# Copies of the forgetting heads from ScalarE to GpSimd, and one row tile's count from VectorE to ScalarE

## The chip, the cores and the metric

The kernel runs on one core of one Trainium2 chip. The metric is the time of one execution on the device in microseconds (us), lower is better. The engines are TensorE (PE in the profile, its weight loads PEld), VectorE (DVE), ScalarE (ACT), GpSimd (POOL) and SyncE (SP), which issues most DMAs.

## The reference

One decoder block on a sequence of 1024 rows of width 1024. The input is normalised and modulated, and one large projection of it gives queries, keys and values of eight forgetting heads and eight sparse heads, an indexer, and two gates. The forgetting heads are causal attention with a decay, the sparse heads attend to 256 keys that the indexer selects, and a gated merge and an MLP follow.

```python
h = rmsnorm(x, g_norm1) * (1.0 + scale1) + shift1
proj = h @ w_in
...
    s = jnp.einsum('bqhd,bkhd->bhqk', qb, k).astype(jnp.float32) * scale
    s = s + Fb[..., :, None] - Ft[:, :, None, :]
    s = jnp.where(mask[None, None], s, -jnp.inf)
    p = jax.nn.softmax(s, axis=-1).astype(v.dtype)
...
    iscore = jnp.where(causal[None], iscore, -jnp.inf)
    _, sel = lax.top_k(iscore, topk)        # topk = 256
...
merged = (jax.nn.sigmoid(gate_fox) * (y_fox @ w_branch_fox)
          + jax.nn.sigmoid(gate_dsa) * (y_dsa @ w_branch_dsa))
x = x + gate1 * (merged @ w_out)
x = x + gate2 * (jnp.square(jax.nn.relu(h2 @ w_mlp1)) @ w_mlp2)
```

## The kernel before

Every product is made from operands split in two halves: a high half `hi`, the value rounded to TensorE's fast 32-bit format, and a low half `lo`, the rest. Three matmuls (`hi*hi`, `hi*lo`, `lo*hi`) stand for one. Weights come by DMA into a staging tile `st` (three buffers), and `split_st` makes `whi` (a copy, L117, on ScalarE) and `wlo` (a difference, L118, on GpSimd for most weights). Both have two buffers.

After a first stage (normalisation, transposes, the indexer's scores), a loop runs over sixteen heads, eight forgetting heads (`n < NH`) and then eight sparse ones. Each turn has the head's `attention`, the next head's projection `proj_qk`, every second turn the values of two heads (`proj_v`), and one or two gate tiles (`gate_tile`), which are 48 matmuls of 128x512 each and fill TensorE between the steps of attention. In `proj_qk` a product of 512 columns in a PSUM bank `g` holds 64 rows of the query and 64 of the key. The score needs the query's high half twice (upper and lower 64 partitions of `QA`), and the key's high half in `KA` and in `KB`: ScalarE makes four copies of 64x512 from the bank (L308, L309, L312, L313), and VectorE the two differences (L310 `QB`, L314 `KA`), of which the last frees the bank.

In the turns of the forgetting heads the kernel also finds the 256th largest indexer score of each row, by 32 steps of bisection (`bisect_step`, four per turn in the code) and one extra count between the two halves of the bits. A step takes a candidate threshold (`cand`, `nct`), counts for each of six row tiles (2 to 7, of 384 to 1024 columns) how many scores reach it, compares (`cnt` with `goal`, L507) and updates the threshold. `count` gives the last `NA` row tiles to ScalarE (L484, a sign with an accumulated sum) and the others to VectorE (L487). `select_tile` (L516 to L524, VectorE alone, with a scan at L521) then makes the masks that the sparse heads need.

Tiles, buffers and semaphores are managed by a framework. It also sets the order on each engine: a planner places the instructions by the program's order of priorities and its own costs, so an instruction stands in its engine's queue where the planner expects it to be ready, and each queue is then worked off in order. Changed costs or engines therefore move the instructions of a whole stage. SyncE's DMA queue is fed in the same way.

Of the kernel before, what the change touches and what calls it, by code (L numbers as in the profile page):

```python
# [9 lines left out]
F32 = mybir.dt.float32  # L10
# [6 lines left out]
AF = mybir.ActivationFunctionType  # L17
# [8 lines left out]
NTT = S // P  # L26
HD = 64
NH = 8
# [29 lines left out]
def block_kernel(ctx: ExitStack, tc: tile.TileContext, x, c, w_ada, b_ada, g_norm1, w_in, b_forget,  # L58
                 rel_bias, w_bf, w_bd, w_out, g_norm2, w_mlp1, w_mlp2, g_final, onehot, out):
    nc = tc.nc  # L60
# [3 lines left out]
    def pool(stack, name, bufs=1, **kw):  # L64
        if kw.get("space") != DRAM:
            kw.setdefault("reuse_waits", "tile")
        return stack.enter_context(tc.tile_pool(name=name, bufs=bufs, **kw))
# [37 lines left out]
    R_d = drm.tile([2, D], F32, name="R_d")  # L105


    def split_w(pieces, lo_eng=None, kt=KT, dst=None):
        st = stg.tile([P, 1024], F32, name="st", tag="st")
        view = st.rearrange("p (k c) -> p k c", k=kt)  # L110
        for d0, d1, src in pieces:
            nc.sync.dma_start(view[:, :, d0:d1], src)
        return split_st(st, lo_eng, dst)

    def split_st(st, lo_eng=None, dst=None):
        hi, lo = dst or [wts.tile([P, 1024], F32R, name=n, tag=n) for n in ("whi", "wlo")]
        nc.scalar.activation(hi, st, AF.Copy)  # L117
        (lo_eng or nc.vector).tensor_tensor(lo, st, hi.bitcast(F32), op=ALU.subtract)  # L118
        return hi, lo

# [70 lines left out]
    with ExitStack() as st1:  # L191
# [38 lines left out]
        with tc.high_priority():  # L230
            for kb, (kt0, n) in enumerate(KBS):
                if kb:
                    was = load_ada(kt0, n)
                for j, wt in was:
                    acc = p1.tile([P, 256], F32, name="acc", tag=f"acc{j}")[:, 0:n * P]
                    if j == 1 and kb < 2:
                        ps = ppv.tile([P, 512], F32, name="pv", tag="pv")
# [17 lines left out]
                for k in range(kt0, kt0 + n):  # L255
                    for g in range(2):
                        gs = slice(g * 512, (g + 1) * 512)
                        ps = ptr.tile([P, 512], F32, name="xT", tag="tr")
# [35 lines left out]
    def proj_qk(kind, h):  # L294
        cq, ck = (C_QF, C_KF) if kind == 0 else (C_QD, C_KD)
        cq, ck = cq + h * HD, ck + h * HD
        hi, lo = split_w([(0, 64, win[:, :, cq:cq + HD]), (64, 128, win[:, :, ck:ck + HD])], nc.gpsimd)
        QA = pQ.tile([P, S], F32R, name="QA", tag="QA", bufs=2)
        QB = pQ.tile([P, S], F32R, name="QB", tag="QB", bufs=2)
        KA = pQ.tile([P, S], F32R, name="KA", tag="KA", bufs=2)  # L300
        KB = pQ.tile([P, S], F32R, name="KB", tag="KB", bufs=2)
        nc.sync.dma_start(QB[64:68, :].bitcast(F32), E_d[kind * NH + h, 0:4, :].bitcast(F32))
        nc.sync.dma_start(KB[64:68, :].bitcast(F32), E_d[kind * NH + h, 4:8, :].bitcast(F32))
        sc = -(HD ** -0.5)
        for half in range(2):
            sl = slice(half * 512, half * 512 + 512)
            ps = gemm_h(hi, lo, half)
            nc.scalar.activation(QA[0:64, sl], ps[0:64, :], AF.Copy, scale=sc)  # L308
            nc.scalar.activation(QA[64:128, sl], ps[0:64, :], AF.Copy, scale=sc)  # L309
            nc.vector.scalar_tensor_tensor(QB[0:64, sl], ps[0:64, :], sc, QA[0:64, sl].bitcast(F32),  # L310
                                           op0=ALU.mult, op1=ALU.subtract)
            nc.scalar.activation(KA[64:128, sl], ps[64:128, :], AF.Copy)  # L312
            nc.scalar.activation(KB[0:64, sl], ps[64:128, :], AF.Copy)  # L313
            nc.vector.tensor_tensor(KA[0:64, sl], ps[64:128, :], KA[64:128, sl].bitcast(F32), op=ALU.subtract)  # L314
        return QA, QB, KA, KB

# [130 lines left out]


    pA = pool(at_stack, "pA")
    NQ, NA = NTT - 2, 2  # L450
    Thi = pA.tile([P, NQ], F32, name="Thi")
    Tlo = pA.tile([P, NQ], F32, name="Tlo")
    cand = pA.tile([P, NQ], F32, name="cand")
# [263 lines left out]

    for n, (kind, h) in enumerate(heads):
        qk = qk_next
        if h % 2 == 0:  # L720
            V = V_next
        attention(kind, h, qk, V[h % 2], Yd)
        if n + 1 < len(heads):
            qk_next = proj_qk(*heads[n + 1])
        if h % 2 == 1 and n + 1 < len(heads):
            V_next = proj_v(heads[n + 1][0], heads[n + 1][1] // 2)
        for g in GATES.get(n, ()):
            gate_tile(g)
        if n < NH:
            for b in range(4):  # L730
                if bit == 15:
                    bisect_mid()
                bisect_step(bit)
                bit -= 1
        if NH <= n + 1 < 2 * NH:
            ada_later(n + 1 - NH)
        if n == NH - 1:
            for i in range(2, NTT):
                select_tile(i)
        if n == 3:  # L740
            dsa_consts()
        for piece in PIECES.get(n, ()):
            branch_fox(piece)
        if n == 2 * NH - 2:
            h_stack.close()
            pYd = pool(yd_stack, "pYd", side="right")
            Yd = [pYd.tile([P, 4, S], F32R, name=f"Yd{v}") for v in range(2)]
            pY = pool(yd_stack, "pY", side="right")
    for v in range(2):
        load_y(Yd[v], 1, v, range(3), slice(0, S))  # L750
        load_y(Yd[v], 1, v, (3,), slice(0, S), slice(0, 64))
# [10 lines left out]
    for half in range(2):  # L762
        sl = slice(half * 512, half * 512 + 512)
        for cp in range(4):
            hi, lo = split_w([(0, 256, wbv[1][:, :, cp * 256:cp * 256 + 256])], nc.gpsimd, 4)
            hv, lv = hi.rearrange("p (k c) -> p k c", k=4), lo.rearrange("p (k c) -> p k c", k=4)
            for c2 in range(2):
# [5 lines left out]
                ps = bank("q")  # L773
# [217 lines left out]
    with ExitStack() as st5:  # L991
# [108 lines left out]
        ps = run(step_24)  # L1100
# [102 lines left out]
```

## Time and profile before

| what | value |
|---|---|
| median of 3 runs | 1655.07 us (1651.3 to 1658.26) |
| the profiled execution | 1651.19 us, span of its instructions 1649.4 us |
| TensorE busy in the span | 1573.0 us (95%) |
| VectorE busy | 1168.3 us (71%) |
| ScalarE busy | 958.9 us (58%) |
| GpSimd busy | 690.7 us (42%) |
| mean granted TensorE clock | 0.982 of full speed |

The forgetting heads' attention runs from about 153 us, where the first score matmul of head 0 starts, to about 531 us, where that of the first sparse head starts. The ends of matmuls are modelled in the trace, so a high busy share of TensorE doesn't yet mean that it works at its best pace; how many matmuls start in a stretch tells more.

### The profile page before, as it was taken

What the parts mean: (1) busy time and instruction counts of PE and PEld (TensorE: products, weight loads), DVE (VectorE), ACT (ScalarE), POOL (GpSimd) and SP (SyncE); (2) the same over time, 40 slices, a digit from 0 to 9 for tenths busy, and PEclk for the clock granted to TensorE, in tenths of its full rate; (3) what the DMA queues carried; (4) which work ended last, traced back from release to release, by engine and by line L of the source; (5) the groups of instructions that cost most, each with busy time, mean ns of one, the idle gap of its engine ahead of it and who ended that gap; (6) DMA issues with size and microseconds to landing.
All of it is one profiled execution on the core that took longest, in us unless ns stands there. A gap on an engine that the chain in (4) does not pass through costs nothing.

```text
span 1649.4 us, 22813 instructions
## 1 busy us (share of the span) xinstructions
PE 1573.0 (95%) x7585; PEld 1302.1 (79%) x7585; DVE 1168.3 (71%) x2293; ACT 958.9 (58%) x1678; POOL 690.7 (42%) x573
## 2 busy tenths in 40 slices
PE   4989999998889999999999998999999989999998
PEld 3767787786678888888887887888888868888887
DVE  6787999999954566556667546765555475758988
ACT  4467898898467777677763135555454343533433
POOL 3421121121122574756655211777766553334730
PEclk7999999999999999999999999999999989999999
DMA  9221122222232444445778455554444479665862
GB/s 301 78 59 57 45 75 56 51 66 50 75 78 65 127 129 113 122 143 152 267 276 271 157 171 203 161 168 159 148 159 141 179 263 354 228 213 191 269 217 103
DMA packets 223870, 253.02 MB, mean 153 GB/s; under 512 B 49136, under 2 KB 136256, under 8 KB 223752
## 3 DMA queue, kind: packets, MB, share of 16 engines
q1 hardware_dynamic: 215112, 233.73, 44.9%
q10 hardware_dynamic: 8640, 17.83, 2.8%
q8 instruction: 60, 0.98, 0.3%
q14 instruction: 58, 0.48, 0.1%
HBM read 186.48 MB, written 65.03 MB: 152 GB/s over the span
## 4 chain that ended last, share of the span: by engine, by line
PE 71%; DVE 16%; ACT 5%; DMA 3%; issue 3%; POOL 1%; SPq 1%; ACTq 0%; DVEq 0%; POOLq 0%
PE g L75 32%; PE S L75 21%; PE tr L75 8%; PE pv L75 7%; DVE bjunk L487 2%; PE ptr L572 2%; DVE ut L1026 2%; DVE acc L247 1%; ACT eqt L484 1%; DVE sp L552 1%; DVE pl L574 1%; ACT sp L559 1%; DMA gt<-G_d 1%; DVE C L1085 1%; ACT sp L556 1%
## 5 line engine op out<-in xcount | busy, mean ns | idle before, releaser
L118 POOL TENSOR_TENSOR wlo<-st,whi 128x1024 fp32r<-128x1024 f32 x60 | 147.6, 2461 | 304.5 <-ACT whi L117 269.5
L75 PE MATMUL g<-h_hi,whi 128*128 128x512 f32 x656 | 265.3, 404 | 7.7 <-DVE KA L314 5.8
L75 PE MATMUL g<-h_hi,wlo 128*128 128x512 f32 x656 | 263.1, 401 | 0.0
L75 PE MATMUL g<-h_lo,whi 128*128 128x512 f32 x656 | 262.0, 399 | 0.0
L1026 DVE TENSOR_TENSOR ut<-rw,ut 128x1024 fp32r<-128x1024 f32 x112 | 185.6, 1701 | 65.9 <-ACT ut L1025 65.5
L1025 ACT ACTIVATE ut<-rw 128x1024 fp32r<-128x1024 f32 x112 | 112.0, 1051 | 141.9 <-PE pv L75 66.8
L1040 POOL TENSOR_TENSOR rw<-rw 128x1024 f32<-128x1024 f32 x40 | 112.1, 2807 | 132.7 <-DMA rw<-in_w_mlp_dram 120.8
L75 PEld LDWEIGHTS g<-h_hi,whi 128*128 128x128 f32 x656 | 125.4, 191 | 33.4 <-DVE KA L314 3.6
L75 PEld LDWEIGHTS g<-h_hi,wlo 128*128 128x128 f32 x656 | 125.2, 191 | 24.4
L75 PEld LDWEIGHTS g<-h_lo,whi 128*128 128x128 f32 x656 | 125.1, 191 | 23.5
L75 PE MATMUL S<-ut 128*128 128x512 f32 (+1 forms) x576 | 138.3, 384 | 0.0
L75 PEld LDWEIGHTS S<-ut 128*128 128x128 f32 x576 | 106.6, 191 | 21.5 <-DVE ut L1026 0.4
L117 ACT ACTIVATE whi<-st 128x1024 fp32r<-128x1024 f32 x74 | 78.0, 1054 | 70.0 <-PE g L75 21.4
L574 DVE TENSOR_TENSOR pl<-ptr,ph 128x512 fp32r<-128x512 f32 (+1 forms) x160 | 99.4, 630 | 24.2 <-ACT ph L573 19.8
L556 ACT ACTIVATE sp<-sp,mn 128x128 f32<-128x128 f32 (+7 forms) x128 | 98.5, 771 | 30.4 <-DVE mn L552 30.1
L573 ACT ACTIVATE ph<-ptr 128x512 fp32r<-128x512 f32 (+1 forms) x160 | 86.0, 551 | 49.4 <-PE ptr L572 46.8
L559 ACT ACTIVATE sp<-sp,mn 128x128 f32<-128x128 f32 (+7 forms) x128 | 96.8, 770 | 18.4 <-DVE mn L558 18.1
L487 DVE TENSOR_SCALAR_CACHE_REDUCE bjunk<-sel_all,cand 128x384 bf16<-128x384 int16 (+7 forms) x132 | 106.3, 805 | 1.4
L572 PE MATMUL ptr<-ident,sp 128*128 128x128 f32 x576 | 91.7, 275 | 9.4 <-DVE pl L574 9.4
L75 PE MATMUL g<-ut 128*128 128x512 f32 (+1 forms) x384 | 94.7, 382 | 6.3 <-ACT ut L1025 4.6
L75 PE MATMUL pv<-ph,V 128*128 128x256 f32 x320 | 86.4, 290 | 1.7 <-DVE yt L581 0.9
L75 PEld LDWEIGHTS g<-ut 128*128 128x128 f32 x384 | 70.0, 191 | 21.1 <-ACT ut L1025 5.0
(433 smaller groups left out, 3873.7 us busy)
## 6 DMA issues: line engine op xcount, KB each, us to landing
rw<-in_w_mlp_dram SPq DMA_DIRECT2D x72, 512.0 KB
rw<-U_d SPq DMA_DIRECT2D x56, 512.0 KB
wap<-in_w_ada_dram SPq DMA_DIRECT2D x64, 256.0 KB
st<-in_w_mlp_dram SPq DMA_DIRECT2D x32, 512.0 KB
st<-in_w_in_dram SPq DMA_DIRECT2D x26, 512.0 KB
U_d<-cc SPq DMA_DIRECT2D x48, 256.0 KB
st<-in_w_in_dram SPq DMA_DIRECT2D x33, 256.0 KB
G_d<-t SPq DMA_DIRECT2D x32, 256.0 KB
```

The lines of the kernel that those rows point to most:

```text
L75: nc.tensor.matmul(o, l, r, start=start, stop=stop)
L117: nc.scalar.activation(hi, st, AF.Copy)
L118: (lo_eng or nc.vector).tensor_tensor(lo, st, hi.bitcast(F32), op=ALU.subtract)
L487: nc.vector.tensor_scalar(bjunk[:, :(i + 1) * P], sel[i].bitcast(dt), thr[:, q], None, op0=ALU.is_ge, op1=ALU.add, accum_out=cnt[:, q])
L556: nc.scalar.activation(sp[:, :W], sp[:, :W], AF.Exp, bias=mn[:, len(cs) - 1:len(cs)], scale=-1.0, accum_out=mn[:, 2:3])
L559: nc.scalar.activation(sp[:, :W], sp[:, :W], AF.Copy, scale=mn[:, 3:4])
L572: nc.tensor.transpose(tr[:, n * P:(n + 1) * P], pt[s][:, kb * P:(kb + 1) * P], ident)
L573: nc.scalar.activation(ph[:, z:], tr[:, z:], AF.Copy)
L574: nc.vector.tensor_tensor(pl[:, z:], tr[:, z:], ph[:, z:].bitcast(F32), op=ALU.subtract)
L1025: nc.scalar.activation(ut[:, n], t, AF.Copy)
L1026: nc.vector.tensor_tensor(ut[:, n + 1], t, ut[:, n].bitcast(F32), op=ALU.subtract)
L1040: nc.gpsimd.tensor_tensor(o, a, b, op=op)
```

## The change

While the loop is in a forgetting head's turn (`n < NH`), three kinds of copies are made by GpSimd: the weights' high half `whi`, the second copy of the query's high half (`QA[64:128]`) and the copy of the key's high half in `KB`. The last two now read the first copy in SBUF, where ScalarE read the PSUM bank. `NA` becomes 3, so ScalarE counts row tile 5 (768 columns) too, and VectorE three tiles in place of four. `on_pool` is set as a turn begins, ahead of its projections and gates, so the first head's projections, made before the loop, are as they were. In all 23 copies of `whi` and 32 of the 64x512 copies go to GpSimd, and 33 counts go from VectorE to ScalarE.

```diff
--- before.py
+++ after.py
@@ -105,6 +105,8 @@
     R_d = drm.tile([2, D], F32, name="R_d")
 
 
+    on_pool = [False]
+
     def split_w(pieces, lo_eng=None, kt=KT, dst=None):
         st = stg.tile([P, 1024], F32, name="st", tag="st")
         view = st.rearrange("p (k c) -> p k c", k=kt)
@@ -114,7 +116,10 @@
 
     def split_st(st, lo_eng=None, dst=None):
         hi, lo = dst or [wts.tile([P, 1024], F32R, name=n, tag=n) for n in ("whi", "wlo")]
-        nc.scalar.activation(hi, st, AF.Copy)
+        if on_pool[0]:
+            nc.gpsimd.tensor_copy(hi, st)
+        else:
+            nc.scalar.activation(hi, st, AF.Copy)
         (lo_eng or nc.vector).tensor_tensor(lo, st, hi.bitcast(F32), op=ALU.subtract)
         return hi, lo
 
@@ -306,11 +311,17 @@
             sl = slice(half * 512, half * 512 + 512)
             ps = gemm_h(hi, lo, half)
             nc.scalar.activation(QA[0:64, sl], ps[0:64, :], AF.Copy, scale=sc)
-            nc.scalar.activation(QA[64:128, sl], ps[0:64, :], AF.Copy, scale=sc)
+            if on_pool[0]:
+                nc.gpsimd.tensor_copy(QA[64:128, sl], QA[0:64, sl].bitcast(F32))
+            else:
+                nc.scalar.activation(QA[64:128, sl], ps[0:64, :], AF.Copy, scale=sc)
             nc.vector.scalar_tensor_tensor(QB[0:64, sl], ps[0:64, :], sc, QA[0:64, sl].bitcast(F32),
                                            op0=ALU.mult, op1=ALU.subtract)
             nc.scalar.activation(KA[64:128, sl], ps[64:128, :], AF.Copy)
-            nc.scalar.activation(KB[0:64, sl], ps[64:128, :], AF.Copy)
+            if on_pool[0]:
+                nc.gpsimd.tensor_copy(KB[0:64, sl], KA[64:128, sl].bitcast(F32))
+            else:
+                nc.scalar.activation(KB[0:64, sl], ps[64:128, :], AF.Copy)
             nc.vector.tensor_tensor(KA[0:64, sl], ps[64:128, :], KA[64:128, sl].bitcast(F32), op=ALU.subtract)
         return QA, QB, KA, KB
 
@@ -447,7 +458,7 @@
 
 
     pA = pool(at_stack, "pA")
-    NQ, NA = NTT - 2, 2
+    NQ, NA = NTT - 2, 3
     Thi = pA.tile([P, NQ], F32, name="Thi")
     Tlo = pA.tile([P, NQ], F32, name="Tlo")
     cand = pA.tile([P, NQ], F32, name="cand")
@@ -717,6 +728,7 @@
 
     for n, (kind, h) in enumerate(heads):
         qk = qk_next
+        on_pool[0] = n < NH
         if h % 2 == 0:
             V = V_next
         attention(kind, h, qk, V[h % 2], Yd)
@@ -746,6 +758,7 @@
             pYd = pool(yd_stack, "pYd", side="right")
             Yd = [pYd.tile([P, 4, S], F32R, name=f"Yd{v}") for v in range(2)]
             pY = pool(yd_stack, "pY", side="right")
+    on_pool[0] = False
     for v in range(2):
         load_y(Yd[v], 1, v, range(3), slice(0, S))
         load_y(Yd[v], 1, v, (3,), slice(0, S), slice(0, 64))
```

The planner orders every queue anew. Three places show it. The first is GpSimd's queue just ahead of the small copies of `dsa_consts` in the fourth turn. `wlo` is the weights' low half, `ph` and `pl` are zeroed blocks of the attention's probabilities. Before:

```order
L568 MEMSET ph 128x128
L569 MEMSET pl 128x128
L118 TENSOR_TENSOR wlo<-st,whi 128x1024
L568 MEMSET ph 128x128
L569 MEMSET pl 128x128
L118 TENSOR_TENSOR wlo<-st,whi 128x1024
```

With the change (a CAST is the copy, L120 of the weights, L315 of the query, L322 of the key):

```order
L322 CAST KB<-KA 64x512
L120 CAST whi<-st 128x1024
L579 MEMSET ph 128x128
L580 MEMSET pl 128x128
L315 CAST QA<-QA 64x512
L123 TENSOR_TENSOR wlo<-st,whi 128x1024
L322 CAST KB<-KA 64x512
L579 MEMSET ph 128x128
L580 MEMSET pl 128x128
L120 CAST whi<-st 128x1024
L123 TENSOR_TENSOR wlo<-st,whi 128x1024
```

Each `wlo` now has its `whi` ahead of it in the same queue, and the query's and key's copies stand between.

The second place is ScalarE's queue around the projection of the third head (`sp` is a softmax tile, `yt` and `yh` the head's output, `ptr` transposed probabilities). Before:

```order
L308 ACTIVATE QA<-g 64x512
L309 ACTIVATE QA<-g 64x512
L484 ACTIVATE eqt,cnt<-sel_all,nct 128x1024
L556 ACTIVATE sp,mn<-sp,mn 128x1024
L580 ACTIVATE yt<-pv 64x256
L573 ACTIVATE ph<-ptr 128x512 x2
L312 ACTIVATE KA<-g 64x512
L313 ACTIVATE KB<-g 64x512
L484 ACTIVATE eqt,cnt<-sel_all,nct 128x896
L559 ACTIVATE sp<-sp,mn 128x1024
L117 ACTIVATE whi<-st 128x1024
```

With the change:

```order
L313 ACTIVATE QA<-g 64x512
L495 ACTIVATE eqt,cnt<-sel_all,nct 128x896
L567 ACTIVATE sp,mn<-sp,mn 128x1024
L591 ACTIVATE yt<-pv 64x256
L584 ACTIVATE ph<-ptr 128x512
L320 ACTIVATE KA<-g 64x512
L495 ACTIVATE eqt,cnt<-sel_all,nct 128x1024
L584 ACTIVATE ph<-ptr 128x512
L570 ACTIVATE sp<-sp,mn 128x1024
L593 ACTIVATE yh<-yt 64x256
```

The pairs of copies have become single ones, `whi` is gone, and the counts (L484, now L495) come in threes.

The third place is VectorE's queue at one step of the bisection, from its counts to its comparison (`sp,mn<-S` are scores with the mask, `mn` their minimum). Before:

```order
L487 TENSOR_SCALAR bjunk,cnt<-sel_all,cand 128x384
L487 TENSOR_SCALAR bjunk,cnt<-sel_all,cand 128x512
L487 TENSOR_SCALAR bjunk,cnt<-sel_all,cand 128x640
L487 TENSOR_SCALAR bjunk,cnt<-sel_all,cand 128x768
L552 ISA sp,mn<-S,cmask 128x384
L552 ISA mn 128x1
L552 ISA sp,mn<-S,cmask 128x512
L552 ISA mn 128x1
L507 TENSOR_TENSOR cnt<-cnt,goal 128x6
```

With the change:

```order
L498 TENSOR_SCALAR bjunk,cnt<-sel_all,cand 128x384
L498 TENSOR_SCALAR bjunk,cnt<-sel_all,cand 128x512
L498 TENSOR_SCALAR bjunk,cnt<-sel_all,cand 128x640
L563 ISA sp,mn<-S,cmask 128x384
L563 ISA mn 128x1
L563 ISA sp,mn<-S,cmask 128x512
L563 ISA mn 128x1
L592 TENSOR_TENSOR yt<-pv,yt 64x256
L563 ISA sp,mn<-S,cmask,mn 128x256
L563 ISA mn 128x1
L585 TENSOR_TENSOR pl<-ptr,ph 128x384
L518 TENSOR_TENSOR cnt<-cnt,goal 128x6
```

One count has gone, and one more step of attention stands between the counts and the comparison, which needs ScalarE's counts. Over the stage the planner spreads the bisection: before, all 132 counts of VectorE and the first scan of `select_tile` stand ahead of the score rows of head 5; with the change the 99 counts end and the first scan stands two score rows into head 6, and the last scan two rows into head 7 (before, at three quarters of head 5).

## Rows read from the trace of the kernel before

**Rows 1.** Windows: heads 0 to 5, heads 6 and 7 together, the sparse heads.
```profile
core 0: us, PE busy (x) PEld busy (x) DVE busy (x) ACT busy (x) POOL busy (x), PEclk, DMA share, GB/s
153.00:180.00 27.00, 26.62 (x129) 21.97 (x128) 24.36 (x78) 22.98 (x43) 5.71 (x7) 1.00 0.35 99
180.00:238.00 58.00, 54.67 (x281) 45.71 (x280) 53.00 (x160) 53.54 (x103) 8.94 (x13) 0.97 0.21 54
238.00:288.00 50.00, 47.52 (x254) 40.34 (x253) 48.98 (x143) 41.35 (x82) 8.56 (x9) 1.00 0.23 65
288.00:336.00 48.00, 45.84 (x226) 38.21 (x225) 45.33 (x135) 41.55 (x80) 8.43 (x11) 0.96 0.19 51
336.00:388.00 52.00, 49.30 (x257) 40.51 (x255) 46.93 (x155) 47.10 (x94) 13.29 (x46) 1.00 0.27 70
388.00:447.00 59.00, 51.29 (x251) 41.77 (x251) 58.65 (x120) 31.91 (x62) 8.93 (x13) 0.94 0.21 57
447.00:531.00 84.00, 77.38 (x403) 64.13 (x404) 43.86 (x120) 60.63 (x119) 16.34 (x23) 0.98 0.23 62
531.00:855.00 324.00, 321.90 (x1763) 275.87 (x1763) 202.82 (x531) 231.34 (x456) 199.35 (x213) 1.00 0.55 169
```

**Rows 2.** Waits from 153 to 531 us: total us, times, longest us.
```profile
PE ptr L572 <- DVE pl L574: 8.9, 3, 4.1
...
PE S L75 <- DVE mn L552: 6.5, 8, 1.2
...
DVE cnt L507 <- ACT eqt L484: 6.0, 8, 1.3
...
PE g L75 <- DVE KA L314: 5.8, 5, 2.2
```

**Rows 3.** Timeline of VectorE around 287 us: start, duration, line, operation.
```profile
287.22 1.01 DVE L487 TENSOR_SCALAR_CACHE_REDUCE bjunk<-sel_all,cand 128x768 bf16<-128x768 uint16 x1
...
288.16 0.08 DVE L487 DVE_READ_ACCUMULATOR bjunk<-sel_all,cand 128x1 f32 x1
...
288.83 2.01 DVE L507 TENSOR_TENSOR cnt<-cnt,goal 128x6 f32<-128x6 f32 x1
```

**Rows 4.** Groups of ScalarE instructions, 153 to 531 us: busy us, mean ns | idle before.
```profile
L117 ACT ACTIVATE whi<-st 128x1024 fp32r<-128x1024 f32 x22 | 23.1, 1052 | 7.9 <-PE g L75 7.6
...
L484 ACT ACTIVATE eqt<-sel_all,nct 128x1024 bf16<-128x1024 int16 x17 | 19.4, 1138 | 0.1
...
L484 ACT ACTIVATE eqt<-sel_all,nct 128x896 bf16<-128x896 int16 x17 | 17.6, 1034 | 4.6 <-DVE nct L480 4.5
...
L313 ACT ACTIVATE KB<-g 64x512 fp32r<-64x512 f32 x14 | 8.3, 595 | 0.2
```

**Rows 5.** Timeline of ScalarE around 222 us.
```profile
222.57 0.92 ACT L556 ACTIVATE sp<-sp,mn 128x768 f32<-128x768 f32 x1
...
223.49 1.05 ACT L117 ACTIVATE whi<-st 128x1024 fp32r<-128x1024 f32 x1
```

**Rows 6.** Groups of GpSimd instructions over the whole span, one form each.
```profile
L118 POOL TENSOR_TENSOR wlo<-st,whi 128x1024 fp32r<-128x1024 f32 x60 | 147.6, 2461 | 304.5 <-ACT whi L117 269.5 <-PE pv L75 14.5 <-DMA Y_d<-yl 13.8
...
L184 POOL MEMSET st<- 128x1024 f32 x1 | 1.0, 952 | 0.0
...
L689 POOL COPY t<-rbd 8x143 f32<-8x143 f32 x1 | 0.3, 292 | 0.0
```

**Rows 7.** Groups of VectorE instructions, 153 to 531 us, one form each.
```profile
L588 DVE TENSOR_TENSOR yl<-yt,yh 64x256 fp32r<-64x256 f32 x29 | 17.5, 602 | 2.6 <-ACT yh L582 2.6
...
L581 DVE TENSOR_TENSOR yt<-pv,yt 64x256 f32<-64x256 f32 x29 | 11.9, 409 | 4.0 <-ACT yt L580 4.0
...
L507 DVE TENSOR_TENSOR cnt<-cnt,goal 128x6 f32<-128x6 f32 x32 | 9.6, 301 | 6.8 <-ACT eqt L484 6.0
...
L508 DVE SCALAR_TENSOR_TENSOR Thi<-cnt,Thi 128x6 f32<-128x6 f32 x16 | 2.6, 164 | 0.5
```

**Rows 8.** Timeline of GpSimd around 288 us.
```profile
288.40 2.41 POOL L118 TENSOR_TENSOR wlo<-st,whi 128x1024 fp32r<-128x1024 f32 x1 [11.88 <-ACT whi L117]
```


## The prediction

> **What bounds the kernel now.** First the windows by head, to see which engine is full where. From 153 to 447 us (heads 0 to 5) VectorE is busy for 277.3 of 294 us, 94%, and in two windows for 98 and 99% [rows 1]. ScalarE has 238.4 us, 81%, with 92 and 91% in its two fullest windows. In the last window (531 to 855 us, sparse heads) both are far from full and TensorE is busy for 321.9 of 324 us.
>
> Busy time says little of TensorE's pace, so I count its matmuls. In the last window 1763 start in 324 us, 0.184 us each. In the seven windows ahead of it 1801 start in 378 us; at 0.184 us they would take 331. So some 47 us are lost between 153 and 531 us: 24.2 in heads 0 to 4 (235 us for 1147 matmuls), 12.9 in head 5 (59 us for 251) and 9.9 in heads 6 and 7 (84 us for 403) [rows 1]. The mix of widths differs a little, so I hold a second measure beside it: TensorE is idle for 25.4 of the 378 us, and the granted clock is under its upper level of 2.4 GHz in four of the windows (0.94 of it in head 5, after waits), which costs about 0.03 x 58 + 0.04 x 48 + 0.06 x 59 + 0.02 x 84 = 9 us. That is 34 us. The stage can give back 34 to 47 us and no more. Then the waits: TensorE waits there for VectorE above all, for `pl` 8.9 us, for `mn` 6.5, for `KA` 5.8 [rows 2].
>
> **What the change does, part by part.**
>
> *VectorE loses 33 counts of 768 columns.* One holds the engine from 287.22 us to the accumulator's read at 288.16, 0.94 us [rows 3]; 33 make 31 us. Three more updates of `goal` on 128x1 at some 0.16 us, by the small operation of [rows 7], are 0.5 us against it.
>
> *ScalarE gets the 33 counts.* It shows none of 768 columns, but an exponential with accumulated sum over 768 fp32 columns starts at 222.57 and the next instruction at 223.49, 0.92 us [rows 5]. The counts of 896 and 1024 columns take 1.03 and 1.14 us [rows 4], so 0.92 fits the line. That is 30 us. It loses 22 copies of `whi` at 1.05 us and 2 x 14 copies of 64x512 at 0.6 us (L309 repeats the row of L313) [rows 4], 23 + 17 = 40 us. ScalarE comes out some 9 us lighter in the stage, so it isn't the next bound by its sum.
>
> *GpSimd gets 22 copies of 128x1024 and 28 of 64x512 in the stage.* The trace has no such copy. From below, a memset of 128x1024 takes 0.95 us; from above, the two-input difference 2.46 us [rows 6]. The one row that is a copy, 143 columns in 0.29 us, lies on a line with the memset, so I take 1.1 and 0.6 us: 24 + 17 = 41 us more, at the upper end 54 + 34 = 88 us. GpSimd is busy for 70 of the 378 us [rows 1], so it ends at 111, at most 158 us: no bound. The copies are on no path either. `whi` and `wlo` together last 3.5 us, at most 4.9, and a gate tile's 48 matmuls at 0.184 us give them 8.8 us while the other buffer is used. Between a projection's last matmul and the first score that needs its copies, the new order of TensorE has at least 84 matmuls, 15 us. That cover costs nothing; without it each copy would show at its own price. The zeroed `ph` and `pl` stand behind the copies and may come up to 3.5 us later; `pl` had to wait for the engine ahead of it anyhow.
>
> *The bank.* Of the four copies out of a product's bank two leave ScalarE's queue, so VectorE's last difference, L314, can be ready 1.2 us sooner. That is part of TensorE's 5.8 us for `KA`.
>
> *VectorE and GpSimd in each other's way.* This speaks against the change. At 288.83 VectorE's comparison of 128x6 takes 2.01 us, and ends within 0.1 us of GpSimd's `wlo` that began at 288.40 [rows 3, 8]. It isn't alone: 32 comparisons have a mean of 301 ns where the like-sized update L508 has 164, and 29 differences `yl`, two inputs in SBUF, take 602 ns where `yt` with one input in PSUM takes 409 [rows 7]. The excess is 32 x 0.137 + 29 x 0.193 = 10 us, while GpSimd runs 22 differences. If the blocked time goes with the square of GpSimd's durations (a hit is as likely as the instruction is long, and lasts half of it), 22 x 2.46² = 133 grows by 22 x 1.1² + 28 x 0.6² = 37, that is by 28% or 3 us; with copies at the upper end by 22 x 2.46² + 28 x 1.23² = 175, or 13 us. The Trainium skill, "SBUF — State Buffer", "Who interferes with whom", states that VectorE's instructions with two SBUF inputs, and its two-port copies, share a port pair with GpSimd's reads, an exclusive lock in which the second one waits out the first; the 2.01 us agree. Its page "Perfetto Trace Analysis", "Optimizing Scalar/DVE Operations", warns that offloading between these two engines might not help for this reason. By the page alone one could expect that nothing of the 31 us lasts. By the rows the loss is 3 to 13 of them.
>
> *The sum.* VectorE has 31 - 0.5 - 3 = 27 us less. Heads 0 to 4 hold nearly all counts; VectorE's 218.6 us there [rows 1] become 192, TensorE's work is 211 us at the pace of 0.184, and ScalarE's 206.5 us about 198. So TensorE is the bound there and VectorE has 10% to spare. A loss of 24.2 us stays in part, since in-order queues still meet: none is lost at the loads of the last window (VectorE 63%, ScalarE 71%), a tenth at today's. At the 88 and 91% to come I take a quarter of it, 6 us: 18 us gained. In head 5 the loss of 12.9 us is `select_tile`'s. It isn't shortened, only moved over heads 6 and 7, where VectorE has 40 of 84 us free; of the two losses, 22.8 us, I take 4 as gained. Together 22 us. The profiled execution took 1651.2 us, 3.9 below the median of the three runs; 1629 for one like it, 1633 by the median. I say 1631. Everything after 531 us keeps its order but for small shifts, and should only start earlier.
>
> **Rivals.**
>
> *One, more of it.* All three losses nearly vanish, since VectorE's load is now even over the heads. 34 to 47 us are the most; 38 gained, 1615 us. Against it: heads 6 and 7 lose 9.9 us at a VectorE load of 52%, in chains that run through both engines.
>
> *Two, the freed time goes back into waits.* GpSimd's reads block VectorE for 13 us (the upper end above), and the comparisons wait for ScalarE's third count: 0.92 us more at each of 32 is 29 us if nothing covers it. Of 31 us nothing is left, and TensorE waits as before: 1651, or 1645 if the shorter hold on the bank stays. For it: the comparison already waits for ScalarE 8 times, 6.0 us [rows 2]. Against it: the new order puts more attention work between count and comparison.
>
> *Three, slower.* The lockstep of the two engines becomes the bound. A step of bisection now needs three counts in a row on ScalarE, 1.14 + 1.03 + 0.92 us [rows 4, 5], behind softmax work of the same queue, and the comparison holds back all the attention queued on VectorE behind it. If every comparison waits as the 8 do (0.75 us) and 0.92 more, the waits go from 6 to 53 us; 47 against 27 saved is 20 us lost on VectorE, of which TensorE, with gate tiles to fill in, shows some 12: 1663. It decides from about 33 us of such waits on.
>
> **How the numbers follow.** A difference of about 0.5%, 8 us here, is what the measurement of this kernel can tell from no change. Chances: the forecast, 10 to 30 us gained, 0.53; rival one 0.12; rival two 0.22, of which 0.05 just beyond 8 us gained; rival three 0.13. The forecast's own range is 1621 to 1642. The whole reaches from rival one's 1612 to rival two's 1655 and leaves out most of rival three and the tail of one. Faster: 0.53 + 0.12 + 0.05 = 0.70; same 0.17; slower 0.13.
>
> **What would show it.** Right: no VectorE count of 768 columns, VectorE under 90% in the windows of heads 0 to 4, TensorE waiting less than 3 us for `KA`, the first sparse head starting near 509 instead of 531 us, and the rest as long as before. The new copies on GpSimd near 1.1 and 0.6 us. Wrong: copies over 2.5 us, comparisons waiting more than 33 us for ScalarE, `yl` and the comparisons longer than now, or scores waiting for `QA` or `KB` from GpSimd.

## The result, and the profile after

The changed kernel takes 1634.09 us (median of 5 runs, 1632.32 to 1635.96), the kernel before on the same chip 1652.95: ratio 0.9887, 95% interval 0.9874 to 0.99, so 1.1% faster. The profiled execution after has a span of 1632.2 us, 17.2 less than before. The forecast was 1631 us.

First the windows after, at the heads' own starts: heads 0 to 4, then head 5 (368 to 420 us), heads 6 and 7, and 324 us of the sparse heads. They answer to [rows 1].

```profile
156.00:183.00 27.00, 25.44 (x121) 20.61 (x120) 22.31 (x67) 20.27 (x43) 8.06 (x9) 1.00 0.34 98
183.00:239.00 56.00, 54.60 (x297) 46.50 (x296) 43.47 (x132) 52.13 (x104) 16.42 (x22) 1.00 0.22 59
239.00:278.00 39.00, 38.51 (x200) 32.39 (x199) 33.64 (x107) 35.62 (x77) 11.90 (x15) 1.00 0.18 55
278.00:334.00 56.00, 55.09 (x297) 46.82 (x296) 45.53 (x136) 48.93 (x98) 15.24 (x20) 1.00 0.26 66
334.00:368.00 34.00, 34.00 (x182) 29.17 (x182) 28.21 (x91) 31.86 (x70) 16.59 (x51) 1.00 0.30 72
368.00:420.00 52.00, 48.71 (x261) 40.73 (x260) 44.20 (x131) 47.37 (x95) 13.14 (x19) 1.00 0.22 56
420.00:514.00 94.00, 87.19 (x451) 72.98 (x450) 84.88 (x181) 54.44 (x112) 35.17 (x37) 0.98 0.26 73
514.00:838.00 324.00, 321.06 (x1754) 275.27 (x1753) 201.40 (x531) 232.63 (x456) 198.23 (x213) 0.99 0.55 168
```

VectorE is busy for 78 to 86% in heads 0 to 4, where it had 90 to 98% [rows 1]; its fullest window is now that of heads 6 and 7, 90%. By the measure of the prediction (0.184 us for each matmul of a window) 1809 matmuls in 358 us lose 25 us, where 47 were lost: 10.2 in heads 0 to 4 (212 us for 1097; it was 24.2), 4.0 in head 5 (12.9) and 11.0 in heads 6 and 7 (9.9). The count of a window takes in the matmuls that straddle its ends, so seven windows count a few twice. Taken as one window, the stage has 1791 matmuls before and 1795 after, and its loss goes from 48 to 28 us.

The first score of head 0 starts at 155.97 us, 2.5 later than before (153.44), the first one of a sparse head at 514.2 in place of 530.7. The stage between them is 19.1 us shorter (358.2 in place of 377.3), and from there to the end the kernel takes 0.7 us less than it did. So nearly the whole gain lies between 156 and 514 us.

The waits after, 156 to 514 us (total us, times, longest us), to [rows 2]:

```profile
DVE cnt L518 <- ACT eqt L495: 17.1, 23, 1.8
...
PE g L75 <- DVE KA L325: 3.8, 5, 1.5
PE pv L75 <- DVE yt L592: 3.1, 3, 1.6
PE S L75 <- DVE mn L563: 2.9, 4, 1.5
```

The wait of `ptr` for `pl` of 8.9 us is gone, that for `mn` less than half, that for `KA` a third shorter. The comparison now waits for ScalarE 23 times.

GpSimd's new copies, 95 to 514 us (busy us, mean ns | idle before):

```profile
L120 POOL CAST whi<-st 128x1024 fp32r<-128x1024 f32 x23 | 27.6, 1201 | 101.4 <-PE g L75 64.8 <-issue 34.7 <-POOL KB L322 1.5
L322 POOL CAST KB<-KA 64x512 fp32r<-64x512 f32 x16 | 13.0, 810 | 20.6 <-ACT KA L320 20.3
L315 POOL CAST QA<-QA 64x512 fp32r<-64x512 f32 x16 | 10.6, 663 | 73.3 <-ACT QA L313 73.1
```

And VectorE's small instructions of the bisection after, 156 to 514 us; the first two answer to rows of [rows 7]:

```profile
L599 DVE TENSOR_TENSOR yl<-yt,yh 64x256 fp32r<-64x256 f32 x29 | 17.7, 612 | 4.1 <-ACT yh L593 3.9
...
L518 DVE TENSOR_TENSOR cnt<-cnt,goal 128x6 f32<-128x6 f32 x32 | 8.1, 253 | 17.1 <-ACT eqt L495 17.1
...
L516 DVE TENSOR_SCALAR cand<-Tlo 128x6 f32<-128x6 f32 x16 | 7.1, 444 | 0.2
L516 DVE TENSOR_SCALAR cand<-Thi 128x6 f32<-128x6 f32 x16 | 5.7, 358 | 0.3
```

`yl` is about as long as before (612 ns on the mean, 602 before), the comparison is shorter (253, 301 before), but the candidate's update has grown. In the kernel before (153 to 531 us):

```profile
L505 DVE TENSOR_SCALAR cand<-Tlo 128x6 f32<-128x6 f32 x16 | 5.1, 318 | 0.3
...
L505 DVE TENSOR_SCALAR cand<-Thi 128x6 f32<-128x6 f32 x16 | 2.6, 165 | 0.3
```

### The profile page after: what moved, and what is told of

Same layout as the page of the kernel before. It is cut to its first block, busy times and chain, and to the rows that moved or that the text cites. A ratio compares the mean times of both kernels' runs of the same rounds, so it can differ in the third digit from the quotient of the medians.

```text
span 1632.2 us, 22837 instructions
## 1 busy us (share of the span) xinstructions
PE 1565.2 (96%) x7585; PEld 1300.7 (80%) x7585; DVE 1150.7 (71%) x2230; ACT 947.4 (58%) x1689; POOL 747.9 (46%) x628
## 4 chain that ended last, share of the span: by engine, by line
PE 73%; DVE 10%; ACT 9%; DMA 4%; issue 2%; SPq 1%; POOL 1%; ACTq 0%; DVEq 0%; POOLq 0%
PE g L75 31%; PE S L75 24%; PE tr L75 8%; PE pv L75 7%; ACT eqt L495 4%; PE ptr L583 2%; ACT sp L567 1%; DVE acc L252 1%; DMA wap<-in_w_ada_dram 1%; ACT sp L570 1%; ACT ph L584 1%; DVE sp L563 1%; DVE pl L585 1%; DVE isc L434 1%; DMA gt<-G_d 1%
## 5 line engine op out<-in xcount | busy, mean ns | idle before, releaser
L1039 DVE TENSOR_TENSOR ut<-rw,ut 128x1024 fp32r<-128x1024 f32 x112 | 182.0, 1670 | 66.3 <-ACT ut L1038 66.2
L1053 POOL TENSOR_TENSOR rw<-rw 128x1024 f32<-128x1024 f32 x40 | 117.6, 2943 | 125.5 <-DMA rw<-in_w_mlp_dram 114.2
L495 ACT ACTIVATE eqt<-sel_all,nct 128x768 bf16<-128x768 int16 (+5 forms) x99 | 102.5, 1035 | 9.9 <-DVE nct L491 8.5
L122 ACT ACTIVATE whi<-st 128x1024 fp32r<-128x1024 f32 x51 | 53.8, 1055 | 62.3 <-DMA st<-in_w_mlp_dram 18.5
```

Of the source, the lines that this page charges most:

```text
L495: nc.scalar.activation(eqt[:, :(i + 1) * P], sel[i].bitcast(dt), AF.Sign, bias=nct[:, q], accum_out=cnt[:, q])
L1039: nc.vector.tensor_tensor(ut[:, n + 1], t, ut[:, n].bitcast(F32), op=ALU.subtract)
L1053: nc.gpsimd.tensor_tensor(o, a, b, op=op)
```

## The experiments

Theories: A, the count frees VectorE and the copies only make room for it on ScalarE; B, the copies do it, since banks come free sooner; C, the count alone does it. Diffs are against the changed kernel unless it is said otherwise. All ratios are against the kernel before, measured beside each; its medians there lie between 1651.9 and 1652.95 us, so times of different versions can be compared to about 1 us.

### One part at a time

The count alone (no copy on GpSimd):

```diff
-        on_pool[0] = n < NH
+        on_pool[0] = False
```

> The count of row tile 5 goes to ScalarE, all copies stay on ScalarE. Theory A (the count frees VectorE, the copies only make room for it on ScalarE): ScalarE has 238 of 294 us in heads 0 to 5 of the kernel before and gets 30 more, 268, above TensorE's 257 there, so it takes VectorE's place as the full engine: 1645 to 1655 us, 0 to 8 us gained. Theory B (the copies do it, since they free the product's bank sooner and shorten ScalarE's queue): no gain or slower, 1650 to 1660. Theory C (the count alone does it, the copies don't matter): 1632 to 1638.

Measured: 1651.24 us, 0.9995 (0.9986 to 1.0004). The copies alone:

```diff
-    NQ, NA = NTT - 2, 3
+    NQ, NA = NTT - 2, 2
```

> The copies go to GpSimd, ScalarE counts two row tiles as before. Theory A: VectorE stays full (277 of 294 us in heads 0 to 5), only TensorE's wait for KA (5.8 us) can shrink: 1647 to 1653 us. Theory B: most of the gain, 1633 to 1640. Theory C: no change, 1651 to 1656, with GpSimd's reads costing VectorE some 3 us.

Measured: 1653.87 us, 1.001 (1.0002 to 1.0019). The count and the weights' copies, the query's and key's copies back on ScalarE:

```diff
             nc.scalar.activation(QA[0:64, sl], ps[0:64, :], AF.Copy, scale=sc)
-            if on_pool[0]:
+            if False:
...
             nc.scalar.activation(KA[64:128, sl], ps[64:128, :], AF.Copy)
-            if on_pool[0]:
+            if False:
```

> The count and the weights' high halves move, the second query and key copies stay on ScalarE. Theory A: ScalarE has 238 + 30 - 21 = 247 us of work in heads 0 to 5, less than TensorE's 257, so most of the gain: 1635 to 1643 us. Theory B: the bank is held as long as before, little gain, 1648 to 1655. Theory C: 1632 to 1638.

Measured: 1648.83 us, 0.9982 (0.9974 to 0.9991). The count and the query's and key's copies, the weights' copies back on ScalarE:

```diff
-        if on_pool[0]:
+        if False:
             nc.gpsimd.tensor_copy(hi, st)
```

> The count and the second query and key copies move, the weights' high halves stay on ScalarE. Theory A: ScalarE has 238 + 30 - 16 = 252 us in heads 0 to 5, just under TensorE's 257: 1637 to 1646 us. Theory B: the bank is free as early as in the changed kernel: 1633 to 1638. Theory C: 1632 to 1638.

Measured: 1638.51 us, 0.9918 (0.9905 to 0.993).

Neither part alone gains anything, so B, which needs a gain from the copies alone, and C, which needs one from the count alone, fall as they stand. A has two of four: the copies alone are 0.9 us over its range (and in C's), the count with the weights' copies 5.8 us over it (and in B's).

B's reason falls as well. It was that the bank comes free sooner, for which TensorE waits as `g` for `KA`, 5.8 us before [rows 2]. That wait with the count alone, where all four copies stand on ScalarE (155 to 522 us), and with the copies alone (156 to 535 us):

```profile
PE g L75 <- DVE KA L325: 0.3, 1, 0.3
```

```profile
PE g L75 <- DVE KA L325: 6.8, 6, 2.5
```

So it isn't the copies on ScalarE that make TensorE wait for the bank.

The totals hide something, though. The windows of the count alone, first from head 0 to the first sparse head, then on to the first matmul of the output projection:

```profile
155.00:522.00 367.00, 350.68 (x1807) 294.73 (x1806) 288.53 (x833) 323.86 (x638) 69.17 (x120) 0.98 0.24 64
522.00:914.00 392.00, 381.70 (x2013) 323.41 (x2012) 234.57 (x593) 257.86 (x493) 227.14 (x228) 0.98 0.56 174
```

and of the kernel before:

```profile
153.00:531.00 378.00, 352.62 (x1791) 292.64 (x1790) 321.10 (x903) 299.07 (x577) 70.20 (x122) 0.98 0.23 63
531.00:910.00 379.00, 376.24 (x2029) 320.13 (x2029) 242.75 (x586) 253.93 (x489) 227.88 (x226) 1.00 0.58 179
```

In the forgetting heads the count alone gains 11 us and TensorE does 16 more matmuls in them. In the sparse heads, to which no edit was made, it loses 13 us and does 16 fewer. The same two windows of every run, with the loss (us less 0.184 per matmul; 0.184 is the pace of the sparse heads of [rows 1]):

| kernel | forgetting heads, us | matmuls | lost | sparse heads and merge, us | matmuls | lost |
|---|---|---|---|---|---|---|
| before | 378 | 1791 | 48 | 379 | 2029 | 6 |
| changed | 358 | 1795 | 28 | 378 | 2018 | 7 |
| count alone | 367 | 1807 | 35 | 392 | 2013 | 22 |
| copies alone | 379 | 1793 | 49 | 378 | 2022 | 6 |
| count, weights | 364 | 1779 | 37 | 388 | 2039 | 13 |
| count, query and key | 356 | 1793 | 26 | 387 | 2022 | 15 |

These are windows of one profiled execution each, and that of the count alone took 3.3 us more than its median (1654.52), so differences of 3 us or so say little.

The losses in the right half go with the order on TensorE. Compared row by row from the end, the order of the changed kernel is that of the kernel before from within head 11 on, that of the copies alone from within head 9 on; those of the other three differ all the way to the first matmul of the output projection. A selection that runs late isn't what they pay for: in these three `select_tile` ends 8 to 14 us ahead of the first sparse head's first score (513.9 and 522 us with the count alone). A run can't swap the order alone, but a barrier can make it the same.

### The same order behind a barrier

Three kernels (before, count alone, changed), each with

```diff
     for n, (kind, h) in enumerate(heads):
+        if n == NH:
+            tc.strict_bb_all_engine_barrier()
         qk = qk_next
```

make the planner begin anew at the first sparse head. TensorE's order is then the same in all three from its first matmuls on.

> The kernel before with a barrier of all engines at the start of the first sparse head's turn, so that the planner writes the rest anew from there; this kernel and the next two have the same order on TensorE from the barrier on. The barrier drains the engines once. Theory P (the count alone frees as much in the forgetting heads as their stage showed, and the planner's other order of the sparse heads gives it back): 1657 to 1668, 5 to 16 us over the kernel before, and the sparse heads lose what they lost before, 13 us or so. Theory S (ScalarE is full with the count alone, and little is freed): the same number here; this kernel is the base for the next two.

Measured: 1680.28 us, 1.0165 (1.0151 to 1.0179); the drained engines cost 28 us, more than expected.

> The count alone (all copies on ScalarE), with the same barrier. Theory P: 11 to 17 us faster than the kernel before with the barrier, since nothing can be given back behind it. Theory S: within 5 us of it.

Measured: 1666.38 us, 1.0086 (1.0072 to 1.01).

> The changed kernel with the same barrier. Theory P: 18 to 24 us faster than the kernel before with the barrier, thus 4 to 10 us faster than the count alone with it: the copies are worth only that. Theory S: 15 us or more faster than the count alone with the barrier: the copies carry the gain.

Measured: 1661.39 us, 1.0054 (1.0041 to 1.0067). The windows of the kernel before with the barrier,

```profile
154.00:551.00 397.00, 362.63 (x1850) 301.78 (x1848) 331.05 (x922) 306.51 (x594) 81.46 (x137) 0.96 0.20 56
551.00:937.00 386.00, 377.06 (x1969) 319.65 (x1969) 230.43 (x565) 249.01 (x471) 217.23 (x211) 0.97 0.58 180
```

of the count alone with it,

```profile
154.00:537.00 383.00, 356.77 (x1848) 299.21 (x1847) 298.28 (x859) 333.67 (x660) 82.81 (x138) 0.97 0.21 58
537.00:923.00 386.00, 376.16 (x1966) 318.93 (x1966) 230.45 (x564) 248.65 (x471) 216.58 (x210) 0.97 0.59 180
```

and of the changed kernel with it:

```profile
157.00:534.00 377.00, 352.70 (x1845) 296.50 (x1844) 308.03 (x859) 297.56 (x612) 126.69 (x186) 0.98 0.21 59
534.00:919.00 385.00, 375.99 (x1967) 318.71 (x1968) 229.12 (x564) 248.64 (x471) 217.10 (x211) 0.97 0.58 179
```

The second windows are equal, 386, 386 and 385 us. In the first the count alone gains 14 us and the whole change 20, at equal matmuls; by the medians 13.9 and 18.9. So theory P is borne out: the count alone is worth some 14 us. Without the barrier the sparse heads gave them back, and with their order made the same they don't; that it is the order follows so far as the barrier changes nothing else there. The copies add 5.0 us.

Which copies? The barrier with the count and the query's and key's copies:

> The count and the query's and key's copies moved, the weights' copies left on ScalarE, with the barrier ahead of the first sparse head. Against the three kernels with the barrier (1680.3 before, 1666.4 with the count alone, 1661.4 with the whole change): if the weights' copies on GpSimd are worth nothing, 1658 to 1663, as fast as the whole change; if they carry a part of the 5 us between the count alone and the whole change, 1664 to 1667. TensorE's order behind the barrier is the same for all but its first part.

Measured: 1657.19 us, 1.0029 (1.0019 to 1.0039).

```profile
156.00:530.00 374.00, 355.42 (x1844) 300.63 (x1842) 294.38 (x859) 316.45 (x632) 100.87 (x164) 0.97 0.22 59
```

By the medians it is 4.2 us faster than the whole change behind the barrier. The profiled execution is the slowest of the eleven (1662.37 us); behind the barrier it takes 391 us where the other three take 385 or 386, and TensorE's order there is the others' only from some 107 us in. The forgetting heads take 374 us, 3 less than with the weights' copies on GpSimd as well, and VectorE is busy for 294.38 us in place of 308.03. The weights' copies are worth nothing here; they cost VectorE time. The pairs without the barrier agree: VectorE's busy time in the forgetting heads goes from 288.53 to 297.26 us (count alone, count and weights) and from 286.88 to 302.24 (count with query and key, changed). That the whole change without the barrier is still 4.4 us faster than with the weights' copies left on ScalarE (1634.09 and 1638.51) comes, by the table above, from the sparse heads, where the two orders differ.

What do the query's and key's copies bring, if not the bank? Against the count alone behind the barrier they save 9.2 us by the medians, and VectorE waits about as much less for ScalarE's copies. With the count alone behind the barrier (154 to 537 us):

```profile
DVE QB L318 <- ACT QA L317: 8.6, 8, 2.9
...
DVE KA L325 <- ACT KB L324: 3.9, 5, 1.0
```

With the query's and key's copies moved as well (156 to 530 us) the first of these is shorter and the second gone, and TensorE's wait of `ptr` for VectorE's `pl` goes from 9.0 to 0.4 us:

```profile
DVE QB L318 <- ACT QA L313: 2.5, 2, 2.0
```

The traces also show where VectorE's time goes. An estimate from them: the time of each VectorE instruction of the forgetting heads above that of the fastest quarter of its like (same operation, tiles and shape, in all runs), where it is 0.1 us or more. It sums to 20 us before and 31 with the change, and nearly all of it lies in instructions that run beside a GpSimd instruction. Before, 12 beside `wlo` make 19.7 us. With the change 14 beside `wlo` make 24.7, six beside copies of `whi` 4.1, five beside the query's and key's copies 1.8. In every version with the weights' copies on GpSimd `wlo` makes 21 to 27 us, in every other 10 to 20. So about a third of what the weights' copies cost is their own; the rest falls on the differences `wlo`, which were on GpSimd before. Why these meet VectorE more then is not shown.

### More of the copies

Each of GpSimd's new copies made twice (here the weights'; the other two likewise):

```diff
             nc.gpsimd.tensor_copy(hi, st)
+            nc.gpsimd.tensor_copy(hi, st)
```

> The changed kernel with each of GpSimd's new copies made twice in a row (the result is the same): 48 us more work on GpSimd, all of it reads that can hold up VectorE. Theory A (the copies lie beside other work, and the blocking of VectorE is small): 1634 to 1639. Rival (VectorE and GpSimd hold each other up, and this takes much of the gain): 8 us or more slower than the changed kernel, 1642 or more, and VectorE's difference yl and the threshold updates longer than with the change.

Measured: 1667.49 us, 1.0093 (1.0078 to 1.0108), 33 us slower than the changed kernel. That is the rival's time, but its mechanism is too small for it. The window of the forgetting heads, and below it VectorE's threshold updates and `yl`:

```profile
159.00:519.00 360.00, 337.72 (x1710) 281.04 (x1709) 301.93 (x841) 290.06 (x590) 144.55 (x210) 0.96 0.24 63
```

```profile
L602 DVE TENSOR_TENSOR yl<-yt,yh 64x256 fp32r<-64x256 f32 x28 | 16.0, 572 | 1.1 <-ACT yh L596 1.0
...
L522 DVE SCALAR_TENSOR_TENSOR Tlo<-cnt,Tlo 128x6 f32<-128x6 f32 x16 | 4.7, 296 | 0.5
...
L519 DVE TENSOR_SCALAR cand<-Tlo 128x6 f32<-128x6 f32 x16 | 4.4, 277 | 0.3
```

VectorE is busy for 301.93 us, as in the changed kernel (302.24), and `yl` and the candidate's update are shorter than there, only the threshold's update longer. By the estimate above the copies of `whi` lengthen VectorE's work by 10.4 us in place of 4.1, and `wlo` by 20.6 in place of 24.7. But TensorE starts 85 matmuls fewer ahead of the first sparse head in 2 us more, and its order is another one through all the heads. To see whether the reads matter, a memset of the same tile in place of the second copy:

```diff
+            nc.gpsimd.memset(hi.bitcast(F32), 0.0)
             nc.gpsimd.tensor_copy(hi, st)
```

> The changed kernel with a memset of the same tile ahead of each of GpSimd's new copies (the copy overwrites it, the result is the same): about as many more instructions on GpSimd as with the doubled copies, and some 35 us more work, but none of it reads SBUF. Theory P (the doubled copies were slow for the other order that the planner then wrote, since it counts GpSimd's time): slower than the changed kernel too, 1640 to 1665. Theory L (they were slow because GpSimd's reads hold up VectorE): 1633 to 1637. Its order is again another one, so that a result between says little.

Measured: 1646.75 us, 0.9969 (0.9959 to 0.998), with 35 us lost in the forgetting heads (363 us, 1781 matmuls) and 14 behind them (388 us, 2031). Without any added read the time comes out 13 us over the changed kernel, in theory P's range. So reads aren't needed for a loss. But the memsets aren't free for VectorE either: it is busy for 308.84 us in place of 302.24, and by the estimate above 4.4 us of it lie beside memsets of `whi` and `QA`. And GpSimd's queue is longer in itself. That the order is the cause in these two runs is thus argued, not shown, and how much of the 21 us between the two is due to the reads they don't tell, since their orders differ.

### One more count

```diff
-    NQ, NA = NTT - 2, 3
+    NQ, NA = NTT - 2, 4
```

> The changed kernel with four row tiles counted by ScalarE, so that 33 counts of 640 columns (0.87 us on VectorE) leave VectorE and take some 0.8 us each on ScalarE, which is 75 to 94% busy in the windows of heads 0 to 4 with the change. TensorE's order from the sparse heads on is that of the changed kernel, so nothing should be given back there. Theory A (the change is near the balance of the two engines): 1639 to 1655, ScalarE over 95% in two or more of these windows, and the comparisons waiting for ScalarE for 30 us or more. Rival (VectorE is still what holds TensorE): 1622 to 1630.

Measured: 1659.37 us, 1.0041 (1.0028 to 1.0053). Theory A gave the sign, but neither the size nor the place. ScalarE is at 94 to 95% in its four fullest windows, comparisons wait for it for 26.4 us, and yet the forgetting heads are the fastest of all, with 16 us lost. The loss is behind them, 45 us:

```profile
155.00:503.00 348.00, 342.93 (x1806) 289.78 (x1806) 244.57 (x729) 315.42 (x657) 108.44 (x169) 1.00 0.24 64
503.00:918.00 415.00, 388.41 (x2010) 325.69 (x2009) 280.06 (x635) 255.94 (x493) 236.08 (x228) 0.97 0.53 168
```

The expectation took TensorE's order there to be that of the changed kernel. By the traces it isn't: compared from the end, 3208 of the 7585 matmuls agree, none of them ahead of the output projection. So a part of the 45 us can be the order's again. Another part is seen directly in VectorE's timeline with four counts: the last comparison of the bisection, the first instruction of `select_tile`, its last.

```profile
487.22 0.15 DVE L518 TENSOR_TENSOR cnt<-cnt,goal 128x6 f32<-128x6 f32 x1
489.13 0.59 DVE L527 TENSOR_SCALAR_CACHE_REDUCE bjunk<-sel_all,Tlo 128x384 bf16<-128x384 uint16 x1
...
559.34 0.92 DVE L535 TENSOR_SCALAR sel_all<-bjunk 128x1024 bf16<-128x1024 bf16 x1
```

The same three in the changed kernel,

```profile
430.04 0.17 DVE L518 TENSOR_TENSOR cnt<-cnt,goal 128x6 f32<-128x6 f32 x1 [1.54 <-ACT eqt L495]
430.79 0.60 DVE L527 TENSOR_SCALAR_CACHE_REDUCE bjunk<-sel_all,Tlo 128x384 bf16<-128x384 uint16 x1
...
496.32 3.19 DVE L535 TENSOR_SCALAR sel_all<-bjunk 128x1024 bf16<-128x1024 bf16 x1
```

and before:

```profile
391.42 0.33 DVE L507 TENSOR_TENSOR cnt<-cnt,goal 128x6 f32<-128x6 f32 x1
392.19 0.61 DVE L516 TENSOR_SCALAR_CACHE_REDUCE bjunk<-sel_all,Tlo 128x384 bf16<-128x384 uint16 x1
...
451.87 0.41 DVE L524 TENSOR_SCALAR sel_all<-bjunk 128x1024 bf16<-128x1024 bf16 x1
```

Each count given to ScalarE makes the bisection end later: 391, 430, 487 us (451 with the count alone, where ScalarE also has all the copies). The first sparse head's masks come out of `select_tile`. Before, it ended 78 us ahead of that head's first score; with the change 15 us (499.5 and 514.2); with four counts it begins 13 us ahead of it and ends 58 us behind it (502.5). The first score needs no mask yet: the last mask is first read 118, 53 and 3 us after it is made. In these stretches of the kernel with four counts

```profile
503.00:525.00 22.00, 16.12 (x73) 12.21 (x72) 21.94 (x44) 13.49 (x26) 20.29 (x17) 0.92 0.46 129
525.00:545.00 20.00, 17.34 (x94) 14.45 (x93) 19.94 (x28) 7.83 (x17) 6.21 (x7) 1.00 0.25 78
545.00:565.00 20.00, 15.51 (x73) 11.91 (x71) 20.00 (x44) 10.15 (x20) 8.49 (x8) 0.91 0.54 157
```

VectorE is never idle, since most of the selection now falls beside the head's own work, and TensorE starts some 240 matmuls in 62 us, where 0.184 us each would be 44: 18 us lost. In the first 62 us of its sparse heads the changed kernel has 346. The other 27 us lie behind, and how much of them the order costs was not settled.

### The first turn's copies left on ScalarE

```diff
-        on_pool[0] = n < NH
+        on_pool[0] = 0 < n < NH
```

> The changed kernel with the first turn's copies on ScalarE, as before; the order of the queues hardly changes behind it. With the change the first score of head 0 starts 2.6 us later than before. If GpSimd's copies in the first turn do that: 1631 to 1633, first score at 154 us or earlier. If it is the order of the queues alone: 1634 to 1636.

Measured: 1626.02 us, 0.9843 (0.9829 to 0.9856): the fastest version here, its interval clear of the changed kernel's. But neither sentence foresaw it. The first score of head 0 comes at 155.0 us, 1.0 of the 2.5 us earlier, so the first turn's copies are a part of that delay at most; with the count alone, where GpSimd has no copy, it comes at 155.1. Another 2 to 3 are gained in the forgetting heads (356 us for 1799 matmuls) and 2 behind them (376 us for 2020), with the same order (7015 of TensorE's 7585 matmuls, counted from the end, thus from the first scores of head 0 on). What these come from was not settled.

## Why the prediction was right

**The bound and the size.** VectorE held TensorE in heads 0 to 4, and lightening it gave back some 20 us between head 0 and the sparse heads, where 22 were forecast (21.8 by the seven windows, 20 by the one). The total is nearer than its parts, and that is luck. Heads 0 to 4 gave back 14.0 (18 predicted), heads 5 to 7 gave back 7.8 (4 predicted), and the two errors cancel. In heads 0 to 4 VectorE was busy for 173 us and ScalarE for 189, less than the 192 and 198 of the sum, and yet 10 us stayed lost and not 6: the rule from loads to losses isn't borne out.

**VectorE's term was mis-sized.** It was to be 27 us lighter; it is 18.9 lighter in the stage (321.10 to 302.24 us busy). The 33 counts are gone, so some 12 us came back where 3 were taken for the two engines in each other's way, close to the upper bound of 13. Of the rows named for it `yl` hardly shows it and the comparison is shorter; the candidate's update does (7.7 to 12.8 us). The 9 to 15 us by which VectorE's busy time grows with the weights' copies, in three pairs of runs, put it at their door; the square rule of the prediction gave those about 2 us. By the overlaps only 4.1 us lie beside these copies themselves and 5.0 more beside `wlo`. The rule also started from 10 us of blocked time, where all kinds of instructions together have 20. That the two engines hold each other up was right; the base and the growth were not.

**ScalarE's term was right.** 9 us lighter predicted, 8.4 measured (299.07 to 290.63). **GpSimd's copies** cost 1.04 us at the median and 0.61 (1.20, 0.66 and 0.81 on the mean), predicted 1.1 and 0.6, and TensorE's matmuls don't wait for one; a single weight load waits 1.5 us for `KB`. But the parts aren't worth what the sum suggests: the 23 us of weights' copies taken from ScalarE gain nothing, the 17 us of query's and key's copies gain 9 at the barrier (383 to 374).

**The bank.** TensorE was to wait less than 3 us for `KA`: it waits 3.8, where it was 5.8. The step's reason fails too. With all four copies on ScalarE and the count moved the wait is 0.3 us, with the copies moved and the count left 6.8.

**The order of the sparse heads.** "Everything after 531 us keeps its order but for small shifts": the time behind the first sparse score is the same to 0.7 us, and TensorE's order is that of before from within head 11 on (ahead of it, in heads 8 to 10, it is another one, at hardly any cost). That holds only by luck, for the prediction gave no reason for it: of the part versions only the one without the count kept it, and the other three lost 7 to 16 us more there. The sum was right about the time because that step was.

**Rival two and three.** The comparisons wait for 17.1 us, between the 6 of before and the 33 from which rival three was to decide. With four counts they reach 26.4 and the forgetting heads are still faster. What the prediction lacked is where `select_tile` may end: it moved it "over heads 6 and 7" as a gain, and had no step for what happens when it runs into the first sparse head. With the change 15 us of room are left.

**Not foreseen:** 2.5 us lost ahead of head 0. They are half of why the first sparse head starts at 514 and not near 509; the other half is that the stage became 19.1 us shorter and not 22.

## What to carry to other kernels

When an engine is relieved of one part of a serial chain, ask where the chain ends now and what its last links run into: with three counts on ScalarE the selection ended 15 us ahead of the first sparse head, with four it ran into that head, which lost 18 us in 62, in a kernel 25 us slower. Where a planner writes the order, a time is that of an edit and of an order: run the parts behind a barrier that makes the rest the same before calling a part worthless, and look in the trace whether it does. And try each of several moved copies by itself; here the largest by time brought nothing.

## What the runs showed of the hardware

A GpSimd copy of 128x1024 fp32 takes 1.04 us at the median of 23 and up to 3.0 us beside VectorE. The longest, in GpSimd's timeline of the changed kernel (start, duration):

```profile
101.24 3.00 POOL L120 CAST whi<-st 128x1024 fp32r<-128x1024 f32 x1 [0.68 <-PE g L75]
```

It began 0.12 us after VectorE's scan with two inputs in SBUF, and ended 0.84 us after it. VectorE's timeline there:

```profile
101.12 2.28 DVE L402 TENSOR_TENSOR_SCAN F<-F 8x1024 f32<-8x1024 f32 x1 [0.92 <-ACT F L401]
```

VectorE's instructions with one input were lengthened too: the update of 128x6 from 318 and 165 to 444 and 358 ns on the mean. The last step of a selection, 0.41 us on 1024 columns before, takes 3.19 us in the row at 496.32 shown above. It began 0.51 us after a `wlo` began on GpSimd and ended 0.86 us after that one's end:

```profile
495.81 2.84 POOL L123 TENSOR_TENSOR wlo<-st,whi 128x1024 fp32r<-128x1024 f32 x1 [5.21 <-DMA isc<-Y_d]
```

Before the change one such step, of 640 columns, took 2.98 us, also beside a `wlo`, so which instruction is hit differs from kernel to kernel. The counts with an accumulator stayed: 873 and 872 ns at 640 columns before, 874 and 873 with the change, and of the 25 that ran beside a `wlo` or a copy with the change none was longer by more than 0.02 us. The Trainium skill, "SBUF — State Buffer", "Who interferes with whom", says that copies and `tensor_scalar`, except in the form that also writes out its accumulator, can use both port pairs where their operands allow it and so collide with GpSimd, and that the one that issued first makes the other wait. These rows agree with it in both points. Why VectorE's work grows by 9 to 15 us with the 23 weights' copies, more than the 3 to 4 us that lie beside them, and changes by only -4 to +5 with 32 copies of 64x512, is not settled. That each `whi` on GpSimd now stands right ahead of its `wlo` may be the reason; no run tests it.
